# A hybrid decoder block on one core: a weight's low part moved to GpSimd, the gated product's low parts ahead of another's, gates in two groups

## The chip, the core and the metric

The kernel runs on one core of one Trainium2 chip. The core has five engines that work side by side: TensorE (PE in the profile) multiplies matrices into PSUM banks, VectorE (DVE) and ScalarE (ACT) do elementwise work, GpSimd (POOL) does elementwise work and starts DMAs, SyncE (SP) only starts DMAs. Each engine takes its own instructions strictly in the order of its queue, and semaphores hold an instruction until what it needs is there. The metric is the time of one execution on the device in microseconds (us); lower is better.

## What is computed

One decoder block on 512 tokens of width 1024, all in float32. A norm and one wide input matrix give the inputs of two branches and their gates; each branch's output is multiplied with a sigmoid gate and the two are merged; an output matrix, a second norm and a squared-ReLU network follow.

```python
h = rmsnorm(x, norm1_g[layer])
proj = h @ w_in[layer]
u, v_g, q, k, v, q_idx, k_idx, w_idx, gates = split_cols(proj, IN_SIZES)
y_a = sgu_mixer(gelu(u), gelu(v_g), w_s[layer], b_s[layer], sgu_ln_g[layer], sgu_ln_b[layer])
...                                   # rope on q, k, q_idx, k_idx; y_b: top-128 sparse attention, 8 heads
g = jax.nn.sigmoid(gates.reshape(B, S, N_BRANCHES, D_MODEL))
merged = g[:, :, 0, :] * (y_a @ w_out_a[layer]) + g[:, :, 1, :] * (y_b @ w_out_b[layer])
x = x + merged @ w_o[layer]
h2 = rmsnorm(x, norm2_g[layer])
x = x + jnp.square(jax.nn.relu(h2 @ w_ff_in[layer])) @ w_ff_out[layer]
return rmsnorm(x, norm_f_g)
```

## The kernel before

**Products in three matmuls.** Every float32 operand is split into a high part (a copy rounded to the matmul's type, on ScalarE, L51) and a low part (what the rounding left, on VectorE or GpSimd, L52); `split` does both. A product is then three matmuls per block of 128 rows: high times low (L148), low times high (L149), high times high (L150); `gemm` issues them. One product of a [128, 512] result over 8 blocks is 24 matmuls, over 4 blocks 12.

**Weights stream through in a fixed order.** `w_plan` numbers all weight tiles in the order of use. A tile n is loaded into one of two buffers `wr` by `w_load`, split into `wh` and `wl` (three buffers each) by `w_conv`, which also starts the next load, and used by `w_get`. `w_ahead(n)`, called at a product's first step, converts up to tile n + 2. The low parts of the tiles named in `POOL_LO` (before: 3 to 23) are made on GpSimd, the others on VectorE. Loads from tile 24 on are started from SyncE's queue. Tiles 20 and 21 belong to the first four heads' k, 22 and 23 to their q, 24 to 27 to `oa` (one tile serves two of its eight products), 40 to 43 to `ob`, 44 to 51 to the output matrix (`wo`).

**What sets the order.** The program is written down with generators: `todo` holds products from which `fill(n)` takes n steps wherever TensorE would have to wait, `later` puts an evacuation some steps after its product. A scheduler of the framework then places each engine's instructions by its own estimate of when their inputs are ready, so the written order is not the final one; `tc.keep_in_program_order` pins an instruction behind everything that is written before it for its engine.

**The places that matter here.**

- *Gated product.* VectorE finds the top 128 of the scores `sc` in 16 rounds (MAX8 L524, MATCH_REPLACE8 L526) and turns the result into a mask (three TENSOR_SCALARs, L531). Then it ropes the first k (L334 to L339, results `k_T`, from where GpSimd's queue copies them into `kq` by DMA, L356), multiplies the gate into `u` (L566) and, after TensorE has transposed `u` (`yt`, L575), makes the high part `yaTh` on ScalarE (L576) and the low part `yaTl` on VectorE (L577), four each. `oa` needs them: its second matmul is L149 on the first `yaTl`.
- *Merge.* ScalarE makes the eight sigmoids of the second gate in place (`z1`, the tiles `zb`, L715). `branch_b` multiplies them with `ob` (L731), adds the first branch (L732) and splits the sum into `mT` (L51, L52), the input of `wo`. Eight `ob` products of 12 matmuls run through the weights 40 to 43.
- *Second norm.* `residual` sums squares on ScalarE while the first two hidden products run (`f`); GpSimd takes the power -1/2 (L200), TensorE spreads the factor over the partitions (`bcast_r2`, the tile `pr`, L801), and the first hidden products are evacuated with it.

Of the kernel before, what the change touches and what calls it, by code (L numbers as in the profile page):

```python
# [12 lines left out]
AF = mybir.ActivationFunctionType  # L13
ALU = mybir.AluOpType
# [4 lines left out]
KD = D // P  # L19
# [14 lines left out]
def hybrid_block_kernel(ctx: ExitStack, tc: tile.TileContext, A: dict, out: bass.AP):  # L34
    nc = tc.nc
    ACT, DVE, POOL, PE = nc.scalar, nc.vector, nc.gpsimd, nc.tensor
# [7 lines left out]
    def bank(name, tag="ps"):  # L44
        return ps.tile([P, 512], F32, tag=tag, bufs=4, name=name)

    def f32(ap):
        return ap.bitcast(F32)

    def split(hi, lo, src, eng=None):  # L50
        ACT.activation(hi, src, AF.Copy)  # L51
        (eng or DVE).tensor_tensor(lo, src, f32(hi), op=ALU.subtract)  # L52


    def unit(tag, dt, name):
        bufs = dict(kq=6, T=3)[tag]
        return E.tile([P, 2, S], dt, tag=tag, bufs=bufs, name=name)

    def half(tag, bufs, name):
        pool, dt = (G, F32) if tag == "yb" else (E, FR)  # L60
        return pool.tile([P, 4, S], dt, tag=tag, bufs=bufs, name=name)

    def tmp(name):
        return G.tile([P, S], F32, tag="ab", bufs=4, name=name)
# [4 lines left out]
    def tick():  # L69
        for d in due:  # L70
            d[0] -= 1
        while due and due[0][0] <= 0:
            due.pop(0)[1]()
# [4 lines left out]
    def fill(n):  # L78
        while n > 0 and todo:
            try:  # L80
                next(todo[0])
                n -= 1
                tick()
            except StopIteration:
                todo.pop(0)

    def run(*gens):
        for g in gens:
            for _ in g:
                tick()  # L90

    def flush():
        while due:
            due.pop(0)[1]()


    wsrc = []
    state = dict(l=0, c=0)
    wraw, wtile = {}, {}
    POOL_LO = range(3, 24)  # L100
    SP_LOAD = 24

    def w_load(eng=None):
        n = state["l"]
        eng = eng or (nc.scalar if n < SP_LOAD else nc.sync)
        if n < len(wsrc):
            wraw[n] = G.tile([P, 1024], F32, tag="wr", bufs=2, name=f"wr{n}")
            eng.dma_start(wraw[n], wsrc[n])
            state["l"] += 1

    def w_conv():
        n = state["c"]
        if n < len(wsrc):
            if n >= state["l"]:
                w_load()
            h = G.tile([P, 1024], FR, tag="wh", bufs=3, name=f"wh{n}")
            l = G.tile([P, 1024], FR, tag="wl", bufs=3, name=f"wl{n}")
            split(h, l, wraw.pop(n), POOL if n in POOL_LO else DVE)
            wtile[n] = (h, l)
            state["c"] += 1  # L120
            w_load()
# [10 lines left out]
        return h.rearrange("p (a b) -> p a b", b=b), l.rearrange("p (a b) -> p a b", b=b)  # L132

    def w_ahead(n):
        while state["c"] < min(n + 3, len(wsrc)):
            w_conv()

    def w_plan(src):
# [3 lines left out]
    def gemm(dst, get, ah, al, evac, lag=1, t0=0):  # L142

        wh, wl, n = get()
        K = len(ah)
        for k in range(K):
            bh, bl = ah[k][:, t0:], al[k][:, t0:]
            PE.matmul(dst, wl[:, k], bh, start=(k == 0), stop=False)  # L148
            PE.matmul(dst, wh[:, k], bl, start=False, stop=False)  # L149
            PE.matmul(dst, wh[:, k], bh, start=False, stop=(k == K - 1))  # L150
            if k == 0 and n is not None:
                w_ahead(n)
            if k == K - 1:
                later(evac, lag)
            yield
# [77 lines left out]
    for k in range(KD):  # L233
        if k == 0:
            h = G.tile([P, 1024], FR, tag="wh", bufs=3, name="wah0")
            l = G.tile([P, 1024], FR, tag="wl", bufs=3, name="wal0")
        elif k < 4:
            h, l = [unit("kq", FR, f"wa{c}{k}").rearrange("p a b -> p (a b)") for c in "hl"]
        elif k < 6:
            t = E.tile([P, 13, P], FR, tag="pt", bufs=2, name=f"wa{k}").rearrange("p a b -> p (a b)")  # L240
            h, l = t[:, :NA], t[:, NA:2 * NA]
        elif k == 6:
            h, l = [unit("T", FR, f"wa{c}{k}").rearrange("p a b -> p (a b)") for c in "hl"]
        else:
            h = unit("T", FR, "wah7").rearrange("p a b -> p (a b)")
            l = E.tile([P, 592], FR, tag="p", bufs=3, name="wal7")
# [69 lines left out]
    for n in range(3):  # L316
        w_conv()
    for j in range(NT):
        rj = rstd[:, j:j + 1]
        for n in range(2):  # L320
            src = acc[j][n][:, :256].rearrange("p (h d) -> p h d", d=64)
# [78 lines left out]
    for n in range(2):  # L400
        b = bank(f"kti{n}", "pa")
# [157 lines left out]
    yaT = [half("ybt", 2, f"yaT{c}") for c in "hl"]  # L559
    for g in range(4):  # L560
        b = bank(f"sg{g}", "pa")
        c = slice(g * P, (g + 1) * P)
# [8 lines left out]
    for g in range(4):  # L571
        fill(1)
        b = bank(f"yt{g}", "pa")
        for c in range(NT):
            tc.keep_in_program_order(PE.transpose(b[:, c * P:(c + 1) * P], u[:, c, g * P:(g + 1) * P], ident))  # L575
        ACT.activation(yaT[0][:, g], b, AF.Copy)  # L576
        DVE.tensor_tensor(yaT[1][:, g], b, f32(yaT[0][:, g]), op=ALU.subtract)  # L577
    while todo:
        fill(8)

# [12 lines left out]
    z1, z1t = [], []  # L593
# [117 lines left out]
    flush()  # L711


    for m in range(KD):
        tc.keep_in_program_order(ACT.activation(z1[m], z1[m], AF.Sigmoid))  # L715
    mT = []

    def hl_tile(n, name):
# [7 lines left out]
    def branch_b(m):  # L726
        b = bank(f"ob{m}", "ps" if m % 2 else "pa")

        def evac():
            t = z1[m]  # L730
            DVE.tensor_tensor(t, b, t, op=ALU.mult)  # L731
            DVE.tensor_tensor(t, t, mA[m], op=ALU.add)  # L732
            h, l = hl_tile(m, f"mT{m}")
            split(h, l, t)
            mT.append((h, l))
        yield from gemm(b, W_OB[m], [ybs["h"][:, k] for k in range(4)], [ybs["l"][:, k] for k in range(4)], evac)

    gens = [branch_b(m) for m in range(KD)]
    for g in gens[:2]:
        for _ in range(3):  # L740
            next(g)
            tick()
    run(*gens)
    flush()

    h2h = [G.tile([P, S], FR, tag="hTh", bufs=KD, name=f"h2h{k}") for k in range(KD)]
# [51 lines left out]
    def bcast_r2():  # L798
        b = bank("pr2", "pa")
        for j in range(NT):  # L800
            PE.transpose(b[:, j * P:(j + 1) * P], rstd2[:, j:j + 1].to_broadcast([P, P]), ident)  # L801
        ACT.activation(R2, b, AF.Copy)
# [42 lines left out]
    def hidden(t, res=None, lag=1):  # L845

        b = bank(f"f1_{t}")

        def evac():
            n, e = t // 2, t % 2  # L850
            plain = n >= 2 * (NG - 1)
            if e == 0:
                o = F.tile([P, 7, 2, SH], FR, tag="f", bufs=3, name=f"fp{n}")
                fpair[n] = dict(o=o)
            fp = fpair[n]
            o = fp["o"]
            r, f = tmp(f"fr{t}"), tmp(f"ff{t}")
            DVE.scalar_tensor_tensor(r, b, 0.0, R2, op0=ALU.max, op1=ALU.mult)  # L858
            ACT.activation(f, r, AF.Square)
            if plain:  # L860
                v = o.rearrange("p a b c -> p (a b c)")
                h, l = v[:, 2 * e * S:(2 * e + 1) * S], v[:, (2 * e + 1) * S:(2 * e + 2) * S]
                ACT.activation(h, r, AF.Square)
                DVE.tensor_tensor(l, f, f32(h), op=ALU.subtract)
                fp[e] = (h, l)
                return
            if e == 0:
                fp["f"] = f
                s = fp["s"] = F.tile([P, 4, SH], F32, tag="s", bufs=1, name=f"fs{n}")
                ACT.activation(o[:, 0, 0], r[:, :SH], AF.Square)  # L870
                DVE.tensor_tensor(o[:, 0, 1], f[:, :SH], f32(o[:, 0, 0]), op=ALU.subtract)
                DVE.tensor_tensor(s[:, 0], f[:, :SH], f[:, SH:], op=ALU.subtract)
                split(o[:, 1, 0], o[:, 1, 1], s[:, 0])
            else:
                fa, s = fp["f"], fp["s"]
                v = f.rearrange("p (a b) -> p a b", a=2)
                ACT.activation(o[:, 2:4, 0], r.rearrange("p (a b) -> p a b", a=2), AF.Square)
                DVE.tensor_tensor(s[:, 1], fa[:, SH:], f[:, SH:], op=ALU.add)
                DVE.tensor_tensor(s[:, 2], s[:, 1], fa[:, :SH], op=ALU.subtract)
                DVE.tensor_tensor(s[:, 3], f[:, :SH], s[:, 2], op=ALU.subtract)  # L880
                DVE.tensor_tensor(o[:, 2:4, 1], v, f32(o[:, 2:4, 0]), op=ALU.subtract)
                split(o[:, 4:7, 0], o[:, 4:7, 1], s[:, 1:4])
        for _ in gemm(b, W_F1[t], h2h, h2l, evac, lag):
            tick()
            if res is not None:
                next(res, None)
# [148 lines left out]
    for _ in res:  # L1035
        pass
    hidden(1, None, 99)
    bcast_r2()
    flush()
    hidden(2)  # L1040
    hidden(3)
    for g in range(NG - 1):
        hidden(4 * g + 4)
# [95 lines left out]
```

## Time and profile before

| | us |
|---|---|
| median of 3 runs | 703.71 (703.55 to 703.91) |
| profiled execution, own time | 703.93 |
| its span, first to last instruction | 702.2 |
| PE busy | 688.3 (98%) |
| DVE busy | 561.9 (80%) |
| ACT busy | 333.9 (48%) |
| POOL busy | 120.5 (17%) |

The profile is of one execution. Its span lacks the 1.7 us that lie around the instructions. The granted clock of TensorE was 0.996 of full speed over the span. A busy share is an average over stages; which wait ends last at a place is read from the timeline there, and the ends of matmuls are modelled, so starts are what to go by on TensorE.

### The profile page before, as it was taken

The page shows a single profiled execution, that of the slowest core. Times are in us where ns is not written, and L with a number is a line of the kernel's source. Part 1 is how long each engine was busy: PE and PEld are TensorE (multiplying, and loading weights), DVE is VectorE, ACT ScalarE, POOL GpSimd, SP SyncE. Part 2 cuts the span into 40 slices and gives each one's busy share as a digit, 9 for nine tenths or more (in the row PEclk, how much of TensorE's full clock was granted, in tenths as well). Part 3 has the DMA queues.
Part 4 walks back from the last instruction along what each step waited for, and adds up shares of the span by engine and source line. Part 5 has one row for each costly group of instructions (what it writes and reads, how often), then busy time and mean ns, then how long its engine had stood idle before and what let it go on. Part 6 is the DMA issues. An engine that isn't in the chain of part 4 may idle for free.

```text
span 702.2 us, 9032 instructions
## 1 busy us (share of the span) xinstructions
PE 688.3 (98%) x3242; PEld 576.3 (82%) x3242; DVE 561.9 (80%) x1036; ACT 333.9 (48%) x570; POOL 120.5 (17%) x147
## 2 busy tenths in 40 slices
PE   9999999999999999999999999999999999999993
PEld 8998888887888888878887888888888888888883
DVE  5674999999757977686426967889797988979994
ACT  6644634323335545473249765354452625445232
POOL 0044348753810840000000000000000000000001
PEclk9999999999999999999999999999999999999998
DMA  8736122232832751324352232231433233142013
GB/s 323 272 88 197 61 90 91 95 116 81 223 116 63 175 154 61 106 78 162 112 203 69 82 150 91 98 113 60 150 91 119 93 105 104 61 150 91 10 51 119
DMA packets 25820, 82.03 MB, mean 117 GB/s; under 512 B 4656, under 2 KB 6320, under 8 KB 23728
## 3 DMA queue, kind: packets, MB, share of 16 engines
q1 hardware_dynamic: 16944, 48.38, 21.4%
q10 hardware_dynamic: 5760, 26.78, 10.9%
q0 software_dynamic: 3072, 6.30, 3.5%
q8 instruction: 25, 0.41, 0.3%
q14 instruction: 19, 0.16, 0.1%
HBM read 71.48 MB, written 2.10 MB: 105 GB/s over the span
## 4 chain that ended last, share of the span: by engine, by line
PE 82%; DVE 14%; issue 2%; ACT 1%; POOL 0%; POOLq 0%; DVEq 0%; ACTq 0%
PE f L150 8%; PE f L149 8%; PE f L148 8%; PE pp L904 6%; PE pp L903 6%; PE pp L902 6%; PE va L285 4%; DVE sc L526 4%; DVE m L524 3%; PE gb L149 2%; PE gb L150 2%; PE gb L148 2%; PE wo L148 2%; PE wo L149 2%; PE wo L150 2%
## 5 line engine op out<-in xcount | busy, mean ns | idle before, releaser
L51 ACT ACTIVATE wh<-wr 128x1024 fp32r<-128x1024 f32 x88 | 93.2, 1060 | 116.9 <-PE f L150 41.7
L148 PE MATMUL f<-h2h,wl 128*128 128x512 f32 x256 | 100.1, 391 | 0.0
L149 PE MATMUL f<-h2l,wh 128*128 128x512 f32 x256 | 99.7, 390 | 0.0
L150 PE MATMUL f<-h2h,wh 128*128 128x512 f32 x256 | 99.6, 389 | 0.0
L52 DVE TENSOR_TENSOR wl<-wr,wh 128x1024 fp32r<-128x1024 f32 x67 | 81.8, 1223 | 20.6 <-ACT wh L51 20.2
L51 ACT ACTIVATE u<-w2r 128x512 fp32r<-128x512 f32 x98 | 59.4, 628 | 78.0 <-DVE w2r L830 25.6
L903 PE MATMUL pp<-u,fp 128*128 128x512 f32 x196 | 76.2, 389 | 0.0
L904 PE MATMUL pp<-u,fp 128*128 128x512 f32 x196 | 76.2, 389 | 0.0
L902 PE MATMUL pp<-u,fp 128*128 128x512 f32 x196 | 73.0, 389 | 0.0
L52 DVE TENSOR_TENSOR u<-w2r,u 128x512 fp32r<-128x512 f32 x98 | 65.0, 687 | 6.1 <-ACT u L51 6.1
L915 DVE TENSOR_TENSOR P<-pp,P 128x512 f32<-128x512 f32 x84 | 54.7, 688 | 16.9 <-PE pp L904 16.8
L52 POOL TENSOR_TENSOR wl<-wr,wh 128x1024 fp32r<-128x1024 f32 x21 | 52.6, 2503 | 48.3 <-ACT wh L51 46.5
L150 PEld LDWEIGHTS f<-h2h,wh 128*128 128x128 f32 x256 | 48.1, 188 | 10.0
L149 PEld LDWEIGHTS f<-h2l,wh 128*128 128x128 f32 x256 | 48.1, 188 | 9.8
L148 PEld LDWEIGHTS f<-h2h,wl 128*128 128x128 f32 x256 | 48.1, 188 | 9.8
L996 POOL TENSOR_TENSOR fss<-fss,mhalf 128x1 f32<-128x1 f32 x3 | 1.6, 548 | 314.2 <-DVE fss L995 314.2
L903 PEld LDWEIGHTS pp<-u,fp 128*128 128x128 f32 x196 | 36.8, 188 | 7.7
L902 PEld LDWEIGHTS pp<-u,fp 128*128 128x128 f32 x196 | 36.8, 188 | 7.6
L904 PEld LDWEIGHTS pp<-u,fp 128*128 128x128 f32 x196 | 36.8, 188 | 7.6
L356 POOL DMA_DIRECT2D kq<-k_T x64 | 32.1, 509 | 49.9 <-ACT k_T L51 31.2
L51 ACT ACTIVATE fp<-fs 128x256 fp32r<-128x256 f32 (+1 forms) x28 | 17.6, 628 | 25.6 <-DVE fs L880 13.3
L858 DVE SCALAR_TENSOR_TENSOR fr<-f,R 128x512 f32<-128x512 f32 x32 | 22.0, 689 | 8.6 <-PE f L150 7.7
(270 smaller groups left out, 1619.2 us busy)
## 6 DMA issues: line engine op xcount, KB each, us to landing
wr<-in_f SPq DMA_DIRECT2D x36, 512.0 KB, 3.5
w2r<-in_f2p ACTq DMA_DIRECT2D x14, 1024.0 KB, 4.9
wr<-in_wt SPq DMA_DIRECT2D x14, 512.0 KB, 4.3
wr<-in_wt ACTq DMA_DIRECT2D x14, 512.0 KB, 3.5
wr<-in_wuv ACTq DMA_DIRECT2D x8, 512.0 KB, 4.0
kq<-k_T POOLq DMA_DIRECT2D x64, 64.0 KB, 3.1
wr<-in_wo SPq DMA_DIRECT2D x8, 512.0 KB, 3.6
xn<-in_xn SPq DMA_DIRECT2D x2, 1024.0 KB, 8.0
```

The source lines that it names most:

```text
L51: ACT.activation(hi, src, AF.Copy)
L52: (eng or DVE).tensor_tensor(lo, src, f32(hi), op=ALU.subtract)
L148: PE.matmul(dst, wl[:, k], bh, start=(k == 0), stop=False)
L149: PE.matmul(dst, wh[:, k], bl, start=False, stop=False)
L150: PE.matmul(dst, wh[:, k], bh, start=False, stop=(k == K - 1))
L285: PE.matmul(acc[j][n][:, :CUT[n].stop - CUT[n].start], a[:, j * P:(j + 1) * P], b[:, CUT[n]], start=(k == 0 and q == 0), stop=(k == KD - 1 ...
L356: eng.dma_start(f32(dst[32 * c:32 * c + 32, :]), f32(T[o][32 * hh:32 * hh + 32, :]))
L526: DVE.match_replace(out=sc[i], in_to_replace=m8[i], in_values=sc[i], imm_value=TAKEN)
L902: PE.matmul(b[j], fl, u[:, 0], start=(q == 0), stop=False)
L903: PE.matmul(b[j], fh, u[:, 1], start=False, stop=False)
L904: PE.matmul(b[j], fh, u[:, 0], start=False, stop=(q == 1))
L915: DVE.tensor_tensor(sums[name, j], b[j], sums[name, j], op=ALU.add)
```

## The change

Four edits. `POOL_LO` takes in weight 24, so that its low part is made on GpSimd; `w_ahead` converts one tile less ahead at the one step where that would be tile 25, whose conversion is then written behind the four `yaTl` (a new `w_conv()` there), and the `yaTl` and tile 25's low part are pinned to that order. The eight sigmoids become two groups of four: one before `ob`, one after its first two products are written. A `drain` stands in GpSimd's queue before the first group. And the spreading of the second norm's factor is written three steps into the third hidden product and no longer ahead of it.

```diff
     def split(hi, lo, src, eng=None):
         ACT.activation(hi, src, AF.Copy)
-        (eng or DVE).tensor_tensor(lo, src, f32(hi), op=ALU.subtract)
+        return (eng or DVE).tensor_tensor(lo, src, f32(hi), op=ALU.subtract)
...
-    POOL_LO = range(3, 24)
+    POOL_LO = range(3, 25)
...
-            split(h, l, wraw.pop(n), POOL if n in POOL_LO else DVE)
+            lo = split(h, l, wraw.pop(n), POOL if n in POOL_LO else DVE)
+            if n == POOL_LO[-1] + 1:
+                tc.keep_in_program_order(lo)
...
     def w_ahead(n):
-        while state["c"] < min(n + 3, len(wsrc)):
+
+        while state["c"] < min(n + (2 if n + 2 == POOL_LO[-1] + 1 else 3), len(wsrc)):
             w_conv()
...
         ACT.activation(yaT[0][:, g], b, AF.Copy)
-        DVE.tensor_tensor(yaT[1][:, g], b, f32(yaT[0][:, g]), op=ALU.subtract)
+        tc.keep_in_program_order(DVE.tensor_tensor(yaT[1][:, g], b, f32(yaT[0][:, g]), op=ALU.subtract))
+    w_conv()
...
-    for m in range(KD):
-        tc.keep_in_program_order(ACT.activation(z1[m], z1[m], AF.Sigmoid))
+    def gates(ms):
+        for m in ms:
+            tc.keep_in_program_order(ACT.activation(z1[m], z1[m], AF.Sigmoid))
+
+
+    tc.keep_in_program_order(POOL.drain())
+    gates(range(4))
...
-    run(*gens)
+    run(*gens[:2])
+    gates(range(4, KD))
+    run(*gens[2:])
...
     hidden(1, None, 99)
-    bcast_r2()
-    flush()
-    hidden(2)
+
+    def late():
+        yield
+        yield
+        bcast_r2()
+        flush()
+        yield
+
+    hidden(2, late())
```

What the scheduler makes of it, engine by engine, in three places. Names carry buffer numbers, and the changed file's lines stand a few further down (L577 is L580 there).

VectorE ahead of `oa`, before: `wl_1651` and `wl_1681` are the low parts of weights 24 and 25, `k_T` the roped k, `q_a` a step of q's rope.

```order
L338 CAST k_T_1597<-k_a_1606 128x512
L52 TENSOR_TENSOR wl_1651<-wr_1522,wh_1650 128x1024
L339 TENSOR_TENSOR k_T_1598<-k_a_1606,k_T_1597 128x512
L334 TENSOR_TENSOR q_a_1737<-q_1645,cosR 128x512
L52 TENSOR_TENSOR wl_1681<-wr_1552,wh_1680 128x1024
L577 TENSOR_TENSOR yaTl<-yt_1695,yaTh 128x512
L577 TENSOR_TENSOR yaTl<-yt_1705,yaTh 128x512
L577 TENSOR_TENSOR yaTl<-yt_1715,yaTh 128x512
L577 TENSOR_TENSOR yaTl<-yt_1725,yaTh 128x512
L335 TENSOR_TENSOR q_b_1738<-q_1646,sinR 128x512
```

The same place of VectorE now.

```order
L341 CAST k_T_1597<-k_a_1606 128x512
L342 TENSOR_TENSOR k_T_1598<-k_a_1606,k_T_1597 128x512
L337 TENSOR_TENSOR q_a_1737<-q_1645,cosR 128x512
L580 TENSOR_TENSOR yaTl<-yt_1689,yaTh 128x512
L580 TENSOR_TENSOR yaTl<-yt_1699,yaTh 128x512
L580 TENSOR_TENSOR yaTl<-yt_1709,yaTh 128x512
L580 TENSOR_TENSOR yaTl<-yt_1719,yaTh 128x512
L52 TENSOR_TENSOR wl_1727<-wr_1552,wh_1726 128x1024
L338 TENSOR_TENSOR q_b_1738<-q_1646,sinR 128x512
```

Weight 24's low part is gone from here and weight 25's stands behind the four `yaTl`. On GpSimd weight 24's now stands last of the low parts, in front of the copies of k:

```order
L52 TENSOR_TENSOR wl_1519<-wr_1445,wh_1518 128x1024
L52 TENSOR_TENSOR wl_1549<-wr_1480,wh_1548 128x1024
L52 TENSOR_TENSOR wl_1651<-wr_1522,wh_1650 128x1024
L359 DMA kq_1507<-k_T_1597 32x512 x4
L359 DMA kq_1509<-k_T_1598 32x512 x4
```

ScalarE at the merge, before: the two `zb` tiles hold four gates each, `wh_2995`, `wh_3037` and `wh_3079` are the high parts of weights 43, 44 and 45, the `mT` rows the high parts of the merged sum.

```order
L715 ACTIVATE zb_1952<-zb_1952 128x512 x4
L715 ACTIVATE zb_2654<-zb_2654 128x512 x4
L51 ACTIVATE mT_2980<-zb_1952 128x512
L51 ACTIVATE mT_2988<-zb_1952 128x512
L51 ACTIVATE wh_2995<-wr_2869 128x1024
L51 ACTIVATE mT_3012<-zb_1952 128x512
L51 ACTIVATE wh_3037<-wr_2957 128x1024
```

ScalarE at the merge now.

```order
L720 ACTIVATE zb_1952<-zb_1952 128x512 x4
L51 ACTIVATE wh_2996<-wr_2869 128x1024
L51 ACTIVATE mT_2977<-zb_1952 128x512
L51 ACTIVATE mT_2985<-zb_1952 128x512
L720 ACTIVATE zb_2654<-zb_2654 128x512 x4
L51 ACTIVATE wh_3038<-wr_2954 128x1024
L51 ACTIVATE mT_3013<-zb_1952 128x512
```

Weight 43's high part now stands behind four sigmoids, where it stood behind eight and two `mT`. VectorE at the merge, before (`wl_2996` is weight 43's low part):

```order
L731 TENSOR_TENSOR zb_1952<-ob_2991,zb_1952 128x512
L731 TENSOR_TENSOR zb_1952<-ob_3015,zb_1952 128x512
L732 TENSOR_TENSOR zb_1952<-zb_1952,mA_1301 128x512
L52 TENSOR_TENSOR mT_2980<-zb_1952,mT_2980 128x512
L52 TENSOR_TENSOR mT_2988<-zb_1952,mT_2988 128x512
L732 TENSOR_TENSOR zb_1952<-zb_1952,mA_1342 128x512
L52 TENSOR_TENSOR wl_2996<-wr_2869,wh_2995 128x1024
L52 TENSOR_TENSOR mT_3012<-zb_1952,mT_3012 128x512
```

And now (`wl_2997` is weight 43's, `wl_3039` weight 44's):

```order
L740 TENSOR_TENSOR zb_1952<-ob_2992,zb_1952 128x512
L52 TENSOR_TENSOR mT_2977<-zb_1952,mT_2977 128x512
L52 TENSOR_TENSOR mT_2985<-zb_1952,mT_2985 128x512
L52 TENSOR_TENSOR wl_2997<-wr_2869,wh_2996 128x1024
L741 TENSOR_TENSOR zb_1952<-zb_1952,mA_1301 128x512
L740 TENSOR_TENSOR zb_1952<-ob_3016,zb_1952 128x512
L52 TENSOR_TENSOR wl_3039<-wr_2954,wh_3038 128x1024
```

Weight 43's low part moves ahead of three steps on `zb`. On TensorE only the beginning of `wo` differs: the three matmuls of the sixth `mT` in the first `wo` product stand two places later among those of the second. The spreading of the second norm's factor, on TensorE, now reads:

```order
L153 MATMUL f_2_3561<-h2h_3121,wh_3448 128x512
L151 MATMUL f_2_3561<-h2h_3122,wl_3449 128x512
L812 MATMUL pr_3577<-ident,rstd_3437 128x128 x4
L152 MATMUL f_2_3561<-h2l_3130,wh_3448 128x512
L153 MATMUL f_2_3561<-h2h_3122,wh_3448 128x512
```

Before, the four `pr` transposes stood between the same two matmuls, at the same row of TensorE's order: nothing moved there.

## Rows read from the trace of the kernel before

**Rows 1.** Waits view of TensorE: us in total, times, longest.

```profile
PE oa L149 <- DVE yaTl L577: 1.3, 1, 1.3
PE pr L801 <- POOL rstd L200: 0.3, 1, 0.3
PE ob L148 <- DVE wl L52: 0.2, 1, 0.2
```

**Rows 2.** Timeline, TensorE, start of `oa`: start, duration, what, [idle before, releaser].

```profile
171.57 0.39 PE L148 MATMUL oa<-yaTh,wl 128*128 128x512 f32 x1
173.23 0.50 PE L149 MATMUL oa<-yaTl,wh 128*128 128x512 f32 x1 [1.28 <-DVE yaTl L577]
173.57 0.40 PE L150 MATMUL oa<-yaTh,wh 128*128 128x512 f32 x1
```

**Rows 3.** Timeline, VectorE, from the end of the top-k chain to `yaTl`.

```profile
160.70 0.91 DVE L531 TENSOR_SCALAR sc<-sc 128x384 f32<-128x384 f32 x3
...
168.66 0.44 DVE L338 CAST k_T<-k_a 128x512 fp32r<-128x512 f32 x1
169.00 1.24 DVE L52 TENSOR_TENSOR wl<-wr,wh 128x1024 fp32r<-128x1024 f32 x1
...
171.34 1.24 DVE L52 TENSOR_TENSOR wl<-wr,wh 128x1024 fp32r<-128x1024 f32 x1
172.47 2.50 DVE L577 TENSOR_TENSOR yaTl<-yt,yaTh 128x512 fp32r<-128x512 f32 x4
```

**Rows 4.** Timelines of ScalarE and GpSimd: weights 23 and 24, GpSimd's next work.

```profile
150.89 1.07 ACT L51 ACTIVATE wh<-wr 128x1024 fp32r<-128x1024 f32 x1 [2.80 <-PE k L150]
159.05 1.07 ACT L51 ACTIVATE wh<-wr 128x1024 fp32r<-128x1024 f32 x1 [7.09 <-PE k L150]
...
152.09 2.40 POOL L52 TENSOR_TENSOR wl<-wr,wh 128x1024 fp32r<-128x1024 f32 x1 [2.30 <-ACT wh L51]
167.88 1.33 POOL L356 DMA_DIRECT2D kq<-k_T  x2 [13.39 <-DVE k_T L338]
```

**Rows 5.** Timelines of GpSimd and VectorE: low parts on GpSimd beside VectorE's work.

```profile
105.54 2.40 POOL L52 TENSOR_TENSOR wl<-wr,wh 128x1024 fp32r<-128x1024 f32 x1
...
121.35 2.59 POOL L52 TENSOR_TENSOR wl<-wr,wh 128x1024 fp32r<-128x1024 f32 x1
...
106.73 1.49 DVE L514 TENSOR_SCALAR vg<-vg,mv,lr 128x512 f32<-128x512 f32 x1
...
121.66 0.67 DVE L526 MATCH_REPLACE8 sc<-m,sc 128x512 f32<-128x512 f32 x1
122.25 2.23 DVE L518 TENSOR_TENSOR vgl<-vg,vgh 128x512 fp32r<-128x512 f32 x1
```

**Rows 6.** Timelines at the merge: TensorE in `ob`, VectorE's weight 43, ScalarE's sigmoids.

```profile
307.96 0.39 PE L150 MATMUL ob<-ybsh,wh 128*128 128x512 f32 x1
308.53 0.47 PE L148 MATMUL ob<-ybsh,wl 128*128 128x512 f32 x1 [0.18 <-DVE wl L52]
308.84 0.40 PE L149 MATMUL ob<-ybsl,wh 128*128 128x512 f32 x1
...
307.16 1.23 DVE L52 TENSOR_TENSOR wl<-wr,wh 128x1024 fp32r<-128x1024 f32 x1
...
300.44 4.29 ACT L715 ACTIVATE zb<-zb 128x512 f32<-128x512 f32 x8
```

**Rows 7.** Timeline of GpSimd at the second norm.

```profile
374.40 1.04 POOL L200 TENSOR_TENSOR rstd<-rstd,mhalf 128x4 f32<-128x4 f32 x1 [115.04 <-DVE rstd L199]
```

**Rows 8.** First head's scores on TensorE; copies of k, q: issues (ns), landings (us).

```profile
194.25 0.28 PE L625 MATMUL at<-kq,kq 128*128 128x256 f32 x1
...
L356 POOL DMA_DIRECT2D kq<-q_T x2: 498/498/498, 188.6 to 189.2; - x2
...
DMA to landing us min/median/max: 2.9/3.1/3.3
...
DMA to landing us min/median/max: 1.8/3.6/5.2
```

## Prediction

> **What bounds the kernel now.** TensorE does. I read the waits of TensorE first [rows 1]: after the start there are only three in 702 us: 1.3 us in the gated product of the first branch (`oa`), 0.3 us at the transposes that spread the second norm's factor (`pr`) and 0.2 us in the output product of the second branch (`ob`). That view counts idle time after a modelled end, so I read the true loss from the timeline, as the distance of starts: matmuls of this shape start 0.23 us apart when nothing holds them.
>
> - `oa` [rows 2]: the second matmul should start at 171.57 + 0.23 = 171.80 and starts at 173.23, 1.43 lost; the one after it comes 0.34 later instead of 0.23, 0.11 more. Together 1.54.
> - `ob` [rows 6]: 307.96 + 0.23 = 308.19, but 308.53: 0.34, and 308.53 to 308.84 is 0.08 more. Together 0.42.
> - `pr` [rows 7]: the 0.3 us of [rows 1], waiting for GpSimd's power, which ends at 374.40 + 1.04 = 375.44.
>
> So whatever this change does elsewhere, it can win about 1.54 + 0.42 + 0.3, some 2.3 us, and no more, unless it makes TensorE do less work, which it does not.
>
> **Part 1, low parts of the gated product ahead of a weight's.** TensorE's second `oa` matmul waits for the first yaTl, which VectorE starts at 172.47 [rows 3]; TensorE follows 173.23 - 172.47 = 0.76 later. Ahead of it VectorE does two weights' low parts, at 169.00 and 171.34, each of which holds the engine 1.13 (the next step starts 1.13 after it: 171.34 to 172.47). One of them (weight 24) goes to GpSimd, the other (25) goes behind the four yaTl. That takes 2 x 1.13 = 2.26 out. The last low part of k now stands directly behind the cast that feeds it; the cast takes 0.44 and its successor started 0.34 after it (168.66 to 169.00), so waiting for its end costs about 0.14. yaTl would start at 172.47 - 2.26 + 0.14 = 170.35, in time for 171.80, and all 1.54 would be won.
>
> But weight 24's low part now runs on GpSimd, and where it lands matters. Its high part ends on ScalarE at 159.05 + 1.07 = 160.12 [rows 4]. For the weight before, GpSimd started 152.09 - (150.89 + 1.07) = 0.13 after ScalarE, and took 2.40. GpSimd has nothing else until 167.88 (13.39 idle). So it runs from 160.25 to 162.65. At 160.70 VectorE begins three TENSOR_SCALARs on `sc` [rows 3], the last step of the top-k chain, and everything down to yaTl follows them without a pause. What happens in such an overlap [rows 5]: a TENSOR_SCALAR begun at 106.73 ends at 108.22, 0.28 after GpSimd's low part (105.54 + 2.40 = 107.94); a TENSOR_TENSOR with two inputs in SBUF, begun at 122.25, ends at 124.48, 0.54 after GpSimd's at 123.94; while a MATCH_REPLACE8 begun at 121.66 is through in 0.67, long before GpSimd is. The first sort waits until GpSimd is done, the second does not care. No row has exactly the `sc` TENSOR_SCALARs against GpSimd, so the cost lies between 0 and the whole overlap; they are nearest to the row at 106.73, and I take the whole of it. The first of the three would end some 0.25 after 162.65 instead of at about 161.0 (a third of 0.91 after 160.70): 1.85 to 1.9 later, I use 1.85.
>
> The Trainium skill, "SBUF — State Buffer", section "Who interferes with whom", has this as a rule that speaks against the move: a VectorE instruction in a two-port mode (it lists tensor_scalar) and a GpSimd instruction exclude each other, and the one that began first keeps the ports for its whole length. By that rule the 1.85 is lost in full, which is my sum; without it the gain would be the 1.54 of the rival below. The rows at 106.73 and 122.25 agree with it.
>
> So yaTl starts at 170.35 + 1.85 = 172.20, TensorE at 172.96 instead of 173.23: 0.27 won of 1.54. A little may go back: the third product takes over a PSUM bank that the rope of q reads last, and that rope now stands behind weight 25. It ends about 172.20 + 4 x 0.60 + 1.13 + 4 x 0.60 + 0.1 = 178.2 (0.60 being the step of the four yaTl, 2.50 in all); TensorE arrives 0.34 + 22 x 0.23 = 5.4 after 172.96, at 178.3 to 178.4. That is a tie; a miss costs 0 to 0.13, I take 0.07. **Part 1: -0.20, between -1.54 and +0.1.**
>
> What the moved step touches otherwise: GpSimd's copies of k and q stand behind the low part, which ends at 162.65, 5 us before the first can start. Weight 26 is loaded when weight 24's buffer is free, now at 162.7 instead of 170.2, so ScalarE's high part no longer waits for that DMA; weight 27 is loaded some 3 us later (after 175.8 instead of 172.6) and is due in `oa` number 6, about 189. Both are covered by TensorE's `oa` work.
>
> **Part 2, sigmoids in two groups.** Before, ScalarE does all eight sigmoids in one run of 4.29 from 300.44 [rows 6], and VectorE reaches weight 43's low part at 307.16; TensorE wants it at 308.19 and gets it at 308.53. Now four sigmoids stand ahead (half of 4.29, until about 302.6), weight 43's high part follows at once (1.05, to 303.6), and VectorE does its low part behind five steps on z and two low parts of mT. I walked ScalarE and VectorE through the new order with their steps of 0.60 and 1.13: the two mT low parts at 304.2 and 304.8, weight 43's from 305.4 to 306.6, 1.6 before TensorE wants it. The stall goes: **-0.42**. What could be late next: weight 44 (ends 309.0, wanted from 313.6), weight 45 (ends 315.0, wanted 317.7), and the sixth and seventh mT. VectorE has the same work in another order with no idle time of over 0.2 us, so it reaches the sixth `ob` at 315.5 as before, and TensorE's order puts two matmuls more ahead of the sixth mT's low part, so that it is wanted at the same time, not 0.42 sooner. Bounds: 0 (the same wait returns at mT) to -0.42.
>
> **Part 3, the rest.** The drain stands in GpSimd's queue between its last copy (before 260) and the power at 374.40, which came after 115.04 us of idleness [rows 7]. Nobody waits for GpSimd in between; the wait that it adds falls into that idleness: 0, and no row shows how it could be more than some tenths. Moving the spreading of the second factor into the third hidden product does not move it: in the built order the transposes stand between the same two matmuls as before. Its inputs come from ScalarE and VectorE work that hangs on TensorE, so all of it shifts together: **0**, the 0.3 stays.
>
> **Sum.** -0.20 - 0.42 = -0.62 on the profiled execution's own 703.93: 703.3. That execution lies 0.22 above the median of the runs, 703.71, so the forecast for a median is **703.1**.
>
> **The rivals.**
> - *The exclusion does not bite*, because the `sc` steps are of the sort that does not wait, or GpSimd is done earlier: then yaTl starts at 170.35, all of 1.54 goes and 0.42 with it: 703.71 - 1.96 = 701.75. It decides if GpSimd's part ends before about 161.3. For it: no such pair in the trace. Against it: the row at 106.73 is the same operation on the same type. 11%; with part of the overlap, times between.
> - *The copies of q come too late* (slower). VectorE's rope of k is 1.85 later, so GpSimd's chain of 48 copies starts later; the last piece of the first head's q was issued at 189.2 and landed 2.9 later, at 192.1, and TensorE uses it at 194.25 [rows 8]. If the chain slips by more than 2.1 us, TensorE stands at the first attention scores, where all else queues behind. Landings there take 1.8 to 5.2 us, by the weight loads they meet. A slip of the whole 1.85 and a landing 2.8 later than now makes 4.65 - 2.1 = 2.5 lost: 703.7 - 0.6 + 2.5 = 705.6. Against it: the middle of that chain waits for landings, not for VectorE, and the weight load that slowed them at 170 is gone. 4%.
> - *A new order trades one wait for another*: the exclusion is longer, or the merge finds its wait at mT. Nothing won: 703.6 to 704.0. 13%.
>
> **How the numbers follow.** Forecast case 72%, 702.6 to 703.5. The range reaches halfway down to the first rival and up to the third: 702.0 to 703.9; outside are the first rival's full form and the second. A measurement here tells about 0.2% (1.4 us) from no change. Faster by that (under 702.3): the first rival and a little of its partial forms, 0.13. Slower: 0.04. Within: 0.83.
>
> **What would show it.** Right: GpSimd's 22nd low part at about 160.25; the `sc` TENSOR_SCALAR stretched to end near 162.9; yaTl near 172.2 and `oa`'s second matmul near 172.96; no wait in `ob`; the 0.3 at `pr` unchanged. Wrong: yaTl near 170.4 (first rival), a wait of TensorE on the q copies near 194 (second), a wait on mT near 315 to 321 (third), or anything that moves where the drain stands.

## The result: 4.7 us faster, outside the forecast range

The changed kernel takes 698.97 us (median of 6 runs, 698.3 to 699.08), the kernel before 703.69 us (703.37 to 703.91) on the same chip. The ratio is 0.9931 [0.9919, 0.9944]: 4.7 us faster, where I had forecast 0.6 and had put the range's end at 702.0.

The page of the kernel after, its first lines:

```profile
span 697.2 us, 9031 instructions
PE 687.9 (99%) x3242; PEld 575.9 (83%) x3242; DVE 562.1 (81%) x1035; ACT 334.0 (48%) x570; POOL 122.8 (18%) x148
q0 software_dynamic: 3072, 6.30, 3.7%
```

The span fell from 702.2 to 697.2, while TensorE's busy time fell by only 0.4 (688.3 to 687.9). Most of the gain is therefore not in TensorE's work. I split each profiled execution at two instants that both kernels have: the first `oa` matmul and the last matmul of the program. Before it: 171.57 us, then 519.79 from the first `oa` to the last matmul (at 691.36), then 10.84 to the end of the span. After it: 171.39, 519.26 (last matmul at 690.65) and 6.59. So the stretch ahead of `oa`, in which TensorE does the same in both, gives 0.18; the body, where all my terms lie, gives 0.53; and the **tail after the last matmul gives 4.25**. The last matmul, before and after:

```profile
691.36 0.28 PE L946 MATMUL f_last<-wh,fp 128*128 128x256 f32 x1
...
690.65 0.28 PE L957 MATMUL f_last<-wh,fp 128*128 128x256 f32 x1
```

**The body, as forecast.** Waits of TensorE in the kernel after (compare [rows 1]); the one at `ob` is gone:

```profile
PE oa L152 <- DVE yaTl L580: 0.9, 1, 0.9
PE pr L812 <- POOL rstd L203: 0.3, 1, 0.3
```

Timeline of TensorE at `oa` after (compare [rows 2]), of VectorE (compare [rows 3]) and of GpSimd (compare [rows 4]); start, duration, what:

```profile
171.39 0.40 PE L151 MATMUL oa<-yaTh,wl 128*128 128x512 f32 x1
172.71 0.50 PE L152 MATMUL oa<-yaTl,wh 128*128 128x512 f32 x1 [0.93 <-DVE yaTl L580]
173.05 0.39 PE L153 MATMUL oa<-yaTh,wh 128*128 128x512 f32 x1
...
160.55 2.68 DVE L534 TENSOR_SCALAR sc<-sc 128x384 f32<-128x384 f32 x3
163.16 0.67 DVE L337 TENSOR_TENSOR k_a<-k,cosR 128x512 f32<-128x512 f32 x1
...
171.97 2.47 DVE L580 TENSOR_TENSOR yaTl<-yt,yaTh 128x512 fp32r<-128x512 f32 x4
174.37 1.21 DVE L52 TENSOR_TENSOR wl<-wr,wh 128x1024 fp32r<-128x1024 f32 x1
...
160.08 2.40 POOL L52 TENSOR_TENSOR wl<-wr,wh 128x1024 fp32r<-128x1024 f32 x1 [5.75 <-ACT wh L51]
```

Weight 24's low part runs on GpSimd from 160.08 to 162.48. Beside it, the three mask scalars take 2.68 instead of 0.91, and VectorE's next step starts at 163.16, 0.68 after GpSimd is done. The four yaTl start at 171.97 and `oa`'s second matmul at 172.71. Its loss is 172.71 - 171.39 - 0.23 = 1.09 plus 0.11 at the next, 1.20 instead of 1.54.

Timeline at the merge after: TensorE in `ob` (compare [rows 6]), ScalarE's two groups of sigmoids, and TensorE at the first attention scores (compare [rows 8]):

```profile
307.71 0.39 PE L153 MATMUL ob<-ybsh,wh 128*128 128x512 f32 x1
307.93 0.39 PE L151 MATMUL ob<-ybsh,wl 128*128 128x512 f32 x1
...
300.18 2.20 ACT L720 ACTIVATE zb<-zb 128x512 f32<-128x512 f32 x4
302.28 1.04 ACT L51 ACTIVATE wh<-wr 128x1024 fp32r<-128x1024 f32 x1
...
304.27 2.18 ACT L720 ACTIVATE zb<-zb 128x512 f32<-128x512 f32 x4
...
193.47 0.39 PE L153 MATMUL oa<-yaTh,wh 128*128 128x512 f32 x1
193.86 0.35 PE L629 MATMUL at<-kq,kq 128*128 128x256 f32 x1
194.06 0.28 PE L630 MATMUL at<-kq 128*128 128x256 f32 x1
```

The `ob` matmuls now follow each other without a pause (0.22 apart), 0.42 won. At the first scores 0.25 goes back (193.47 to 193.86 is 0.16 too much, 193.86 to 194.06 another 0.09): the copies of q come a little late, the forecast's second rival in a small form. The last of the first head's four was issued at 191.47 and landed 2.0 later, at 193.45 (before: 189.16 and 192.05), and TensorE would have taken it up at 193.70. 0.34 + 0.42 - 0.25 = 0.51, the body's 0.53.

**The tail, which I had not looked at.** The kernel before, of the chain that ended last, three of its last pieces (start, us, what), and the last instructions of GpSimd, SyncE and ScalarE:

```profile
691.31 1.49 issue
692.80 0.71 POOLq L1135
...
693.53 0.72 ACT fo L1027
...
692.83 0.66 POOL L987 TENSOR_TENSOR fss<-fss,mhalf 128x1 f32<-128x1 f32 x1 [1.52 <-DVE fss L984]
...
694.04 0.33 SPq L1028 DMA_DIRECT2D out<-acc  x1
...
694.28 0.35 ACTq L1029 DMA_DIRECT2D out<-fo  x1
```

Nothing of the program's own arithmetic happens after 694.25, and the last output DMA is issued by 694.63; yet the span ends at 702.2. `POOLq L1135` is an instruction of GpSimd's queue at the line where the program ends. The views leave it at 0.71; the trace's own records of instructions give it in full. It is a DRAIN, which every engine has at the end (start, duration, end in us):

```
before   GpSimd  DRAIN  692.80  8.62  701.42   end of program
         Sync    DRAIN  697.17  0.01  697.18   end of program, behind the waits for the output
after    GpSimd  DRAIN  258.25  8.80  267.05   the drain that the change adds at the merge
         GpSimd  DRAIN  692.09  0.76  692.85   end of program
         Sync    DRAIN  696.47  0.01  696.48   end of program, behind the waits for the output
```

Before, SyncE had seen the last output land by 697.18, and then everybody waited 701.42 - 697.18 = 4.24 us longer for GpSimd. After, GpSimd has paid at 258 us, with nothing to do until 373.73, and the end follows SyncE. 4.24 is the tail's 4.25.

### The profile page after: what moved, and what is told of

Its sections match the earlier page's. It is cut to its first block, busy times and chain, and to the rows that moved or that the text cites. A ratio compares the mean times of both kernels' runs of the same rounds, so it can differ in the third digit from the quotient of the medians.

```text
span 697.2 us, 9031 instructions
## 1 busy us (share of the span) xinstructions
PE 687.9 (99%) x3242; PEld 575.9 (83%) x3242; DVE 562.1 (81%) x1035; ACT 334.0 (48%) x570; POOL 122.8 (18%) x148
## 3 DMA queue, kind: packets, MB, share of 16 engines
q0 software_dynamic: 3072, 6.30, 3.7%
## 4 chain that ended last, share of the span: by engine, by line
PE 83%; DVE 13%; issue 1%; ACT 1%; DMA 1%; POOL 0%; SPq 0%; POOLq 0%; DVEq 0%; ACTq 0%
PE f L152 8%; PE f L153 8%; PE f L151 8%; PE pp L914 6%; PE pp L913 6%; PE pp L915 6%; DVE sc L529 4%; PE va L288 3%; DVE m L527 3%; PE gb L152 2%; PE gb L153 2%; PE gb L151 2%; PE wo L153 2%; PE wo L151 2%; PE wo L152 2%; PE pv L660 2%
## 5 line engine op out<-in xcount | busy, mean ns | idle before, releaser
L52 DVE TENSOR_TENSOR wl<-wr,wh 128x1024 fp32r<-128x1024 f32 x66 | 80.3, 1220 | 22.9 <-ACT wh L51 22.6
L52 POOL TENSOR_TENSOR wl<-wr,wh 128x1024 fp32r<-128x1024 f32 x22 | 55.0, 2498 | 53.8 <-ACT wh L51 52.0
```

Of the source, the lines that this page charges most:

```text
L52: return (eng or DVE).tensor_tensor(lo, src, f32(hi), op=ALU.subtract)
```

## The experiments

Theory A: a drain of GpSimd costs so much for the DMAs that GpSimd has issued since the last one, and the change moves that cost from the end into idle time. Rival B: the short drain at the end is a by-product and the moved instructions make the gain. All times are medians; every ratio is against runs of the kernel before on the same chip. The table splits the profiled execution of each kernel as above.

| kernel | first `oa` matmul at | to last matmul | tail | time, us | ratio to before |
|---|---|---|---|---|---|
| before | 171.57 | 519.79 | 10.84 | 703.69 | |
| after | 171.39 | 519.26 | 6.59 | 698.97 | 0.9931 [0.9919, 0.9944] |
| e1 drain alone | 171.01 | 519.77 | 6.58 | 699.11 | 0.9937 [0.9922, 0.9952] |
| e2 no drain | 170.87 | 518.99 | 10.84 | 702.76 | 0.9987 [0.9978, 0.9997] |
| e3 drain after 48 copies | 170.95 | 519.76 | 6.93 | 699.64 | 0.9945 [0.9928, 0.9961] |
| e4 copies on SyncE | 171.44 | 537.71 | 6.47 | 717.54 | 1.0193 [1.0178, 1.0208] |
| e5 drain early | 171.59 | 519.77 | 10.84 | 703.80 | 1.0003 [0.9991, 1.0014] |
| e6 gates undone | 171.18 | 519.40 | 6.58 | 698.90 | 0.9935 [0.9922, 0.9949] |
| e7 low parts undone | 171.11 | 519.39 | 6.57 | 698.82 | 0.9935 [0.9923, 0.9948] |
| e9a masks later | 171.28 | 517.71 | 6.58 | 697.63 | 0.9915 [0.9901, 0.9928] |
| e9 masks and late | 171.62 | 517.35 | 6.58 | 697.23 | 0.9909 [0.9896, 0.9923] |
| e10 copies of q split | 171.54 | 522.85 | 12.14 | 708.37 | one run |

The first column varies by 0.64 us among kernels that are alike up to there (before, e1, e3, e5, e10: 170.95 to 171.59), while the second stays within 0.03 among those whose body differs by a drain at most (before, e1, e3, e5: 519.76 to 519.79). So a body term of some tenths is read from the second column rather than from the median.

### Does the drain make the gain, or the rest?

e1 is the kernel before with one line, ahead of the sigmoids:

```diff
+    tc.keep_in_program_order(POOL.drain())
     for m in range(KD):
         tc.keep_in_program_order(ACT.activation(z1[m], z1[m], AF.Sigmoid))
```

> The kernel before with the drain at the merge and nothing else. Theory A (the end of the program waited for a GpSimd drain of 8.6 us, and a drain at the merge takes that cost where GpSimd is idle): the span's end no longer waits for GpSimd, 703.7 - 4.3 = 699.4 us; the drain at the merge takes about 8.8 us, that at the end about 0.8. Rival B (the gain of 4.7 us comes from the moved low parts and sigmoids, the short drain at the end is a by-product): 703.7 us.

Measured: 699.11, 4.6 us faster than before. The body takes 519.77 as before (519.79), and the tail 6.58. The drain at the merge takes 8.79 and that at the end 0.76.

e2 is the kernel after without that line:

> The kernel after without its drain at the merge; the rest of the change stays. Theory A: the end drain is back at about 8.6 us and the time at 699.0 + 4.3 = 703.3, less what is left of the body's gain, that is 703.0 us (the time that was forecast for the whole change, 703.1). Rival B: 699.0 us.

Measured: 702.76; the end drain is 8.62 again and the tail 10.84, to the hundredth that of before. Rival B falls: the one line is worth 3.8 to 4.6 us by the medians and 4.25 by the tail, with or without the rest, and the rest about 0.9 us by the medians (ratio 0.9987 [0.9978, 0.9997]), 0.80 by the body. 702.76 lies within the range that I had given for the whole change.

### What is in the 8.6 us?

e3 puts the drain in the kernel before into the middle of GpSimd's 96 copies of k and q into `kq`:

```diff
     tc.keep_in_program_order(POOL.memset(f32(ptl[:, 11]), 0.0))
+    tc.keep_in_program_order(POOL.drain())
```

> The kernel before with one drain in the middle of GpSimd's 96 copies into kq: behind the first 48 and the two memsets of pth and ptl. What is the 8.6 us made of? A1 (so much for each copy issued since the last drain, 8.7/96 = 0.09 us each): both drains about 4.4 us; 692.8 + 4.4 = 697.2 is where SyncE's waits for the output end, so about 699.5 us. A2 (a fixed cost whenever there were copies since the last drain): both about 8.7 us, 703.7 us. A3 (the first drain of a program pays it once, whatever stood before): 8.7 us in the middle, 0.8 at the end, 699.4 us.

e4 issues those copies from SyncE instead, with no drain added:

```diff
-            restack(kq[hh][1], T, hh, (0, 1, 0, 1), nc.gpsimd)
-            restack(kq[hh][2], T, hh, (2, 3, 2, 3), nc.gpsimd)
+            restack(kq[hh][1], T, hh, (0, 1, 0, 1), nc.sync)
+            restack(kq[hh][2], T, hh, (2, 3, 2, 3), nc.sync)
...
-            restack(kq[hh][0], T, hh, (0, 1, 2, 3), nc.gpsimd)
+            restack(kq[hh][0], T, hh, (0, 1, 2, 3), nc.sync)
```

> The kernel before with the 96 copies into kq issued by SyncE, none by GpSimd, and no drain added (the order of the first scores moves with it). If the cost belongs to GpSimd's copies (A1, A2): the end drain takes about 0.8 us without any drain before it, and the time is about 699.4 us, give or take 1 us for the moved order and for the waits in SyncE's queue. If it belongs to the first drain as such (A3): 8.6 us at the end, about 703.7 us, give or take the same.

e5 puts the drain ahead of all copies, behind the first mask (`mb0`), in the kernel before:

```diff
                        compare_op=ALU.is_ge, fill=-BIG)
+    tc.keep_in_program_order(POOL.drain())
```

> The kernel before with one drain ahead of all copies into kq (behind GpSimd's first mask, within the first 10 us) and none at the merge. If each copy leaves 0.082 us for the next drain, as the two halves suggest: the early drain is short, that at the end 8.6 us, 703.7 us. If any drain earlier in the program would do: 0.8 us at the end, 699.3 us.

e10 adds no drain and makes more copies of the same bytes: the 16 copies of the second group's q become 32 of half the rows:

```diff
+    def q1_done(T):
+        for hh in range(4):
+            for c in range(4):
+                for r in (0, 16):
+                    nc.gpsimd.dma_start(f32(kq[hh][0][32 * c + r:32 * c + r + 16, :]),
+                                        f32(T[c][32 * hh + r:32 * hh + r + 16, :]))
...
-    todo.append(rope_tiles(W_Q1, "q1", q_done))
+    todo.append(rope_tiles(W_Q1, "q1", q1_done))
```

> The kernel before, no drain added, with the last 16 of GpSimd's 96 copies (q of the second four heads) each in two copies of 16 rows: 112 copies, the same rows and bytes. By the number of copies: end drain 0.76 + 112 x 0.082 = 9.9 us. By rows or bytes: 8.6 us as before. The time is later by the second scores' wait for 16 more issues of 0.5 us on GpSimd, up to 8 us, less what the other work there hides: 704 to 713 us; its size is not what the run is for.

The drains of these kernels, from the trace's instruction records; "behind work" is the drain's end less the end of GpSimd's last own instruction (a power, a memset or the issue of a copy):

| drain | copies since the last one | starts | takes | behind work | for each copy |
|---|---|---|---|---|---|
| before, end | 96 | 692.80 | 8.62 | 701.42 - 693.49 = 7.93 | 0.083 |
| after, merge | 96 | 258.25 | 8.80 | 267.05 - 259.14 = 7.91 | 0.082 |
| after, end | 0 | 692.09 | 0.76 | 692.85 - 692.79 = 0.06 | |
| e3, middle | 48 | 194.28 | 6.15 | 200.43 - 195.48 = 4.95 | 0.103 |
| e3, end | 48 | 692.15 | 4.70 | 696.85 - 692.85 = 4.00 | 0.083 |
| e4, end | 0 | 710.59 | 0.76 | | |
| e5, early | 0 | 1.23 | 0.61 | | |
| e5, end | 96 | 692.80 | 8.62 | as before | 0.083 |
| e10, end | 112 | 695.83 | 9.93 | 705.75 - 696.52 = 9.23 | 0.082 |

So it is A1. A drain costs 0.08 us for each copy that GpSimd has issued since the drain before it. A drain ahead of the copies saves nothing (e5), one in the middle leaves half (e3), a program without such copies has no such end (e4, in its drain), and 112 copies of the same bytes cost 16 x 0.08 more (9.93, expected 9.9). It makes no difference whether the last copy has only just been issued (258 us) or lies 430 us back (692 us). In e3 the half that is left ends at 696.85, just behind SyncE's 696.54, and the tail is 6.93 instead of 6.58. It is the count and not the bytes; but the packets that the page gives for the DMA queue grow in step with the count, 3072 for 96 copies and, in e10,

```profile
q0 software_dynamic: 3584, 6.30, 3.5%
```

which is 32 packets a copy in both. Whether copies or packets are what is paid for stays open. So does the 1 us more of e3's drain in the middle. Copies were still landing then (the last was issued at 194.63 and landed at 198.4), but so they were at the merge of the kernel after (258.64 and 262.2), where the price was the usual 0.082.

The time of e4 is a miss. The drain was as expected and the tail 6.47, but the body grew by 17.9 us. Its TensorE, ScalarE and SyncE at the place (timelines):

```profile
183.70 0.39 PE L150 MATMUL oa<-yaTh,wh 128*128 128x512 f32 x1
194.19 0.79 PE L148 MATMUL oa<-yaTh,wl 128*128 128x512 f32 x1 [10.10 <-DVE wl L52]
194.78 0.63 PE L149 MATMUL oa<-yaTl,wh 128*128 128x512 f32 x1
195.20 0.63 PE L150 MATMUL oa<-yaTh,wh 128*128 128x512 f32 x1
195.63 0.63 PE L148 MATMUL oa<-yaTh,wl 128*128 128x512 f32 x1
...
191.82 1.06 ACT L51 ACTIVATE wh<-wr 128x1024 fp32r<-128x1024 f32 x1 [12.72 <-DMA wr<-in_woa]
...
167.46 20.48 SPq L356 DMA_DIRECT2D kq<-k_T  x32
188.04 1.02 SPq L108 DMA_DIRECT2D wr<-in_woa  x2
```

Weights from number 24 on are loaded through SyncE's queue, which takes its instructions in order. The 32 copies of k hold it from 167.46 to 187.94, two weight loads come behind them, and TensorE stands 10 us for the weight's low part. The rest of the 17.9 is smaller: 12 matmul steps at TensorE's lower clock take 5.27 instead of 2.76 (194.19 to 199.46); the second 32 copies of k hold SyncE from 241.28 to 261.54, the weights behind them come late, and TensorE waits 1.9 more for a low part in the product `gb` and then runs at the lower clock again; and there is a wait of 1.4 at `pt` that the kernel before does not have. I had named "the waits in SyncE's queue" and priced them at 1 us.

### What the two moves are worth by themselves

e6 is the kernel after with the eight sigmoids in one group again, e7 the kernel after with weight 24's low part back on VectorE and weight 25's not held; both keep the drain.

```diff
-    gates(range(4))
+    gates(range(KD))
...
-    run(*gens[:2])
-    gates(range(4, KD))
-    run(*gens[2:])
+    run(*gens)
```

> The kernel after with the second gate's eight sigmoids in one group again; drain and low parts stay. Theory (the second group took away a PE stall of 0.42 us at ob, as forecast): 699.0 + 0.4 = 699.4 us, the stall of 0.3 to 0.5 us between 308 and 309 us back. Rival (with the drain there, the sum of the body's small stalls doesn't reach the end): 699.0 us.

```diff
-    POOL_LO = range(3, 25)
+    POOL_LO = range(3, 24)
...
-        while state["c"] < min(n + (2 if n + 2 == POOL_LO[-1] + 1 else 3), len(wsrc)):
+        while state["c"] < min(n + 3, len(wsrc)):
...
-        tc.keep_in_program_order(DVE.tensor_tensor(yaT[1][:, g], b, f32(yaT[0][:, g]), op=ALU.subtract))
-    w_conv()
+        DVE.tensor_tensor(yaT[1][:, g], b, f32(yaT[0][:, g]), op=ALU.subtract)
```

> The kernel after with weight 24's low part back on VectorE and weight 25's not held behind yaTl; drain and sigmoids stay. Forecast term: +0.20 us, 699.2 us, with the oa stall back from 1.10 to 1.44 us and the stall at the first scores (193.86) gone. Rival (what oa won the later q copies gave back in full at the first scores): 699.0 us. Second rival (all of 0.52 us that oa's second matmul came earlier is lost): 699.5 us.

Measured: 698.90 and 698.82, not to be told from the kernel after; the forecast times of 699.4 and 699.2 did not come, and by the medians alone both rivals at 699.0 would stand. Their profiles do show the terms. e6 has the `ob` stall back (first two rows: 307.18 to 307.75), e7 the one at `oa` (172.78):

```profile
307.18 0.39 PE L153 MATMUL ob<-ybsh,wh 128*128 128x512 f32 x1
307.75 0.47 PE L151 MATMUL ob<-ybsh,wl 128*128 128x512 f32 x1 [0.18 <-DVE wl L52]
...
171.11 0.40 PE L149 MATMUL oa<-yaTh,wl 128*128 128x512 f32 x1
172.78 0.50 PE L150 MATMUL oa<-yaTl,wh 128*128 128x512 f32 x1 [1.28 <-DVE yaTl L578]
```

Against the body of e1 (519.77, drain alone) the sigmoids alone (e7) are worth 0.38 and the low parts alone (e6) 0.37; both together, in e2, 0.78. In the profiled execution of the kernel after they give only 0.51, because that one waits 0.25 for q's copies at the first scores; the profiled executions of e2 and e6, with the same order there, do not. The medians could not show terms of this size: the runs of one kernel lie up to 1 us apart (703.04 to 704.07 for the kernel before).

### Is the stretched mask what holds `oa`?

e9a holds the three mask scalars behind weight 25's low part, where GpSimd has no arithmetic to do:

```diff
-    for i in range(1, NT):
-        DVE.tensor_scalar(sc[i], sc[i], TAKEN, -BIG, op0=ALU.is_gt, op1=ALU.mult)
...
     w_conv()
+    for i in range(1, NT):
+        tc.keep_in_program_order(DVE.tensor_scalar(sc[i], sc[i], TAKEN, -BIG, op0=ALU.is_gt, op1=ALU.mult))
```

> The kernel after with the three mask scalars (L534, stretched from 0.91 to 2.68 us beside GpSimd's low part) held behind weight 25's low part on VectorE. Theory (that stretch is what holds yaTl, and so oa): VectorE reaches the ya chain up to 2.6 us earlier, the oa stall of 1.10 us falls to 0.2 or less, the q copies start about 1 us earlier: 699.0 - 1.0 = 698.0 us. Rival (the ya chain waits for TensorE's transposes and ScalarE's yaTh, which end at 171.5, so the stretch was slack): oa stall stays near 1.0 us, 698.9 us.

Measured: 697.63, and the body 1.55 shorter than after. VectorE and TensorE in e9a:

```profile
160.44 0.68 DVE L337 TENSOR_TENSOR k_a<-k,cosR 128x512 f32<-128x512 f32 x1
...
169.26 1.87 DVE L578 TENSOR_TENSOR yaTl<-yt,yaTh 128x512 fp32r<-128x512 f32 x3
...
173.15 0.89 DVE L581 TENSOR_SCALAR sc<-sc 128x256 f32<-128x256 f32 x3
...
171.28 0.39 PE L151 MATMUL oa<-yaTh,wl 128*128 128x512 f32 x1
171.51 0.40 PE L152 MATMUL oa<-yaTl,wh 128*128 128x512 f32 x1
```

VectorE starts the rope of k at 160.44 instead of 163.16 and yaTl at 169.26 instead of 171.97; the masks, now away from GpSimd's low part, take 0.89. The stall at `oa` is gone, and so is the one at the first scores.

e9 also holds the transposes that spread the second norm's factor behind the fifth step of the third hidden product, with TensorE's order pinned there (the third matmul of each step of that product is pinned too):

```diff
-            PE.transpose(b[:, j * P:(j + 1) * P], rstd2[:, j:j + 1].to_broadcast([P, P]), ident)
+            tc.keep_in_program_order(PE.transpose(b[:, j * P:(j + 1) * P], rstd2[:, j:j + 1].to_broadcast([P, P]), ident))
...
     def late():
         yield
         yield
+        yield
+        yield
         bcast_r2()
```

> As the run with the masks later, and the four transposes of rstd2 (pr, L812) held behind the fifth step of the third hidden product by program order, so that they come 0.5 us or more later on TensorE, after the power on GpSimd (ends 374.77). Theory: the stall of 0.48 us at pr goes as well, 698.0 - 0.45 = 697.5 us. Rival (R comes later, VectorE's first fr and with it the bank of a later hidden product come later: the stall moves): 698.0 us.

Measured: 697.23. The stall at `pr` is gone (373.30 to 373.55):

```profile
373.30 0.39 PE L153 MATMUL f<-h2h,wh 128*128 128x512 f32 x1
373.55 0.65 PE L814 MATMUL pr<-ident,rstd 128*128 128x128 f32 x4
```

In the kernel after, the same place has 0.71 between the two (374.11 to 374.82):

```profile
374.11 0.39 PE L151 MATMUL f<-h2h,wl 128*128 128x512 f32 x1
374.82 0.65 PE L812 MATMUL pr<-ident,rstd 128*128 128x128 f32 x4 [0.32 <-POOL rstd L203]
```

The body is another 0.36 shorter, against 0.45 expected. That is 6.4 us below the kernel before in the same runs (703.63), and below the kernel after; the two medians 697.63 and 697.23 by themselves do not tell e9 from e9a.

## Why the prediction was wrong

**The step that failed is in "What bounds the kernel now".** I read the waits of TensorE, summed them to 2.3 us, and wrote that the change "can win about 1.54 + 0.42 + 0.3, some 2.3 us, and no more". That holds for the time up to the last matmul. It leaves out the 10.84 us behind it, where TensorE has nothing left to wait for and so shows no wait. Of these, 4.24 were GpSimd's end drain alone, and that could be read off the trace before: the span end 7.6 us behind the last issue, the `POOLq` piece in the chain, the drain's record of 8.62 us against SyncE's end at 697.18.

**Part 3, the drain: 0, measured -4.25 on the span.** I priced what the added drain would delay, which is rightly nothing: it runs from 258.25 to 267.05 and GpSimd's next work comes at 373.73. I did not ask what a drain does to a later drain. "No row shows how it could be more than some tenths" was true of the rows that I had picked, not of the trace. Even with the end drain seen, that an earlier one takes its cost was not in the trace; the fair forecast would have had a case of 703.1 - 4.2 = 698.9, and the trace could not have settled its chance. The closing line of the prediction did name "anything that moves where the drain stands" as a sign of error, at the wrong place: what moved was the end.

**The rest of Part 3: right.** The transposes at `pr` did not move, and the stall stayed (374.11 to 374.82 after). With TensorE's order pinned, in e9, they did move and the stall went.

**Part 1, forecast -0.20; measured -0.34 at `oa`, with 0.25 given back at the first scores in one execution and nothing in two others.** The steps came out as worked: GpSimd's low part at 160.08 (160.25 forecast; all here is 0.18 earlier), the masks held until GpSimd was done and 1.77 lost (1.85), yaTl at 171.97 (172.20), `oa`'s second matmul at 172.71 (172.96). The Trainium skill, "SBUF — State Buffer", section "Who interferes with whom", has the rule of the exclusion; the trace agrees (2.68 beside GpSimd, 0.91 and 0.89 without). e9a won 1.55 us of the body, not only the 1.20 left at `oa`, since q's copies come sooner too; but it takes the masks' whole 2.68 out of the way and not the exclusion's 1.77 alone. By estimate the 1.77 alone would have cleared `oa` (171.97 - 1.77 + 0.74 = 170.94, and TensorE wants it at 171.62); no run has the 1.77 by itself. The first rival, that the exclusion does not bite, is out. The give-back of 0.07 at the third product did not show; the second rival, late copies of q, came in small.

**Part 2, forecast -0.42; measured -0.38 to -0.42.** The stall at `ob` went and nothing came in its place.

The body's forecast of -0.62 thus lies between the 0.53 of the profiled execution after and the 0.80 of e2; the whole error is the tail. The range was also not quite what its words say: halfway from 703.1 to the first rival's 701.75 is 702.4, not 702.0. That decides nothing, as 698.97 lies far outside both.

## What to carry to other kernels

Split the span at the last matmul before summing anything: what follows it has its own bound, and the waits of the busiest engine say nothing about it. Compare there, engine by engine, when each is through with its own end; the last one sets the time. If GpSimd issues DMAs, look at how long its end drain takes: here it paid 0.08 us for each of them, so that a drain behind the last copy, in a stretch where GpSimd is idle, took that cost off the end. It has to stand behind the copies, and a few dozen may stay (here (697.18 - 693.49) / 0.083, some 44, by estimate from the rows of before) before the drain is longer than the wait for the output.

## What the hardware showed that I had not expected

- **A drain of GpSimd paid 0.08 us for each DMA that GpSimd had issued since its last drain**, 7.9 us for 96 copies of 32 packets, at once or 430 us later; when there were none it ended 0.06 us behind GpSimd's work. The Trainium skill, "VectorE: DVE Perf Modes", section "The DRAIN you can't avoid", says that the boilerplate drains around a kernel take about 12 ns, constant, on all five engines. The drains here stand at the program's own first and last lines, and whether the skill means these no run shows. Ten of the 17 in the kernel before take 7 to 19 ns; TensorE's and VectorE's first end drains take 2.35 and 0.52 us, most of it while their last work runs, and GpSimd's takes 8.62. For these the measurement decides.
- **In e4 TensorE came out of two pauses at its lower clock.** Windows around the stall at `oa` (window, us; busy times of PE, PEld, DVE, ACT, POOL; granted clock, DMA share, GB/s):

```profile
170.00:182.00 12.00, 10.73 (x49) 8.53 (x49) 9.72 (x16) 2.27 (x4) 0.00 (x0) 1.00 0.43 104
194.30:197.00 2.70, 2.70 (x7) 2.12 (x8) 1.22 (x1) 1.66 (x2) 0.00 (x0) 0.50 0.45 109
197.00:199.00 2.00, 2.00 (x6) 1.56 (x5) 0.00 (x0) 0.00 (x0) 0.00 (x0) 0.50 0.41 100
202.00:205.00 3.00, 3.00 (x15) 2.49 (x14) 0.69 (x1) 0.00 (x0) 0.00 (x0) 1.00 0.55 224
```

  The granted clock is 1.00 (2.4 GHz) ahead of the stall and 0.50 (1.2 GHz) when TensorE resumes at 194.19; matmuls there take 0.63 instead of 0.39 and start 0.43 apart instead of 0.23. It is back at 1.00 by 202. The second pause is shorter: at `gb` TensorE stands from about 268.94 to 270.86, and the granted clock is 0.50 from 271.10 to 274.50 and 1.00 from 274.60 to 280. No run changes a pause alone, so that the pauses are the cause is read from the order of events. In the kernel after, whose longest stall from `oa` to the last matmul is 1.1 us, the page has 9 tenths or more for that clock in each of its 40 slices.
